# Low parts of the weights by an accumulating DMA instead of a DVE subtraction

## The chip, the core and the metric

The kernel runs on one core of a Trainium2 chip. A core has a matrix engine (TensorE, in the profile PE, with its weight loads as PEld), a vector engine (DVE), a scalar engine (ACT), GpSimd (POOL) and a sync engine (SP) that here only issues transfers. Sixteen DMA engines move data between the device memory and the core's working memory (SBUF). The metric is the device time of one execution in microseconds, lower is better.

## The reference

One layer of a decoder with 512 tokens, 16 meta tokens in front, 1024 channels and 8 heads. Two branches run side by side on the same normalised input, differential softmax attention and a gated delta rule in chunks; their results are projected, gated, added and projected once more.

```python
hn = rms_norm(h, norm_w)
proj = hn @ w_in
aq, ak, av, az, dq, dk, dv, dz, db, da, ga, gd = split(proj)
o_a = diff_attention(aq, ak, av, lam)
y_a = (rms_norm(o_a, attn_norm_w) * (1 - lam_init) * silu(az)) @ w_branch_attn
o_d = gated_delta_chunked(q, k, v, beta, g)      # q, k, v: conv + silu of dq, dk, dv
y_d = (rms_norm(o_d, dn_norm_w) * silu(dz)) @ w_branch_delta
merged = sigmoid(ga) * y_a + sigmoid(gd) * y_d
out = rms_norm(h + merged @ w_out, final_norm_w)
```

All of it is in fp32. `w_in`, the two branch matrices and `w_out` are the weights that this document is about.

## The kernel before

**Products.** The large products run on PE in a format with fewer mantissa bits than fp32 (float32r). To keep the accuracy, both factors are split into a high part, which is the value rounded to that format, and a low part, which is the rest, and three passes are added up: high times high, high times low, low times high (`PASSES`, line 54). So each 128 x 1024 block of weights (512 KB) is needed as two tiles, `wh` and `wl`; for the output projection most of them are called `woh` and `wol`. There are 96 blocks in the order of the list `ORDER` (four groups of two heads, then the gates and the branch projections) and 8 blocks of `w_out`.

**How a block is prepared.** `load_weights(n)` (line 404) takes one of the `raw` tiles and lets SP load the block into it. `split(n, raw)` (line 383) then takes a slot for a pair of split tiles and does two things: ACT copies `raw` to `wh`, which rounds it, and DVE writes `wl` as `raw` minus `wh`. With that the raw tile is given back. The table `SLOTS` (line 64) says how many tiles of each kind exist: three `raw`, two pairs `w`, four pairs `wo`. So a block's copy can start when PE has finished with the block two places earlier, and the next load when a subtraction has ended.

**How a block is used.** `dense()` makes the products in `ORDER`. For each eighth of the depth it issues the three passes one behind the other, so the low part of the weights enters with the third matmul of a block (the second in the first two blocks, which are made by `first_products` as the tokens arrive). `give("w")` at its end frees the pair.

**What sets the order.** The kernel does not leave the order to the compiler. Its parts are generators (tasks), and a planner (`Plan`) runs them on a table of estimated times: the task that can start soonest by that estimate emits its next instruction. The result is one fixed order of instructions for each engine; every engine keeps its order and waits at the first instruction that isn't ready. The estimate of a DMA (`transfer`) counts its bytes once, whatever its kind. What stands around the split on the engines: on ACT the copies out of the accumulators, tanh (`th`), the exponentials (`e`) of the softmax and those of the decays (`E`, `eg`); on DVE the delta rule's triangular inverse, a chain of some thirty pairs `tmps`, `ts` in each of the four groups; on POOL masks (`E`, `ts`), small powers and the copies of `ak` within SBUF; on SP the loads of `raw` and small transfers by way of the device memory (`scrm`, `msub`, `scrt`, `td`, `E` and `eg` from `gcd`).

Every engine instruction is emitted by one helper, so nearly all of them have line 216 in the profile; groups are told apart by their tiles.

Of the kernel before, what the change touches and what calls it, by code (L numbers as in the profile page):

```python
# [10 lines left out]
F32 = mybir.dt.float32  # L11
# [25 lines left out]
def dense_order():  # L37
    """Products with weight blocks of 128 columns, in the order in which they are made."""
    order = []
    for g in range(H // 2):  # L40
        for n in ("dk", "dv", "dq"):
            order += [(n, 2 * g), (n, 2 * g + 1)]
        order += [(n, 2 * g) for n in ("ak", "aq", "az", "av")]
        order += [("dz", 2 * g), ("dz", 2 * g + 1)]
        order += [(n, 2 * g + 1) for n in ("ak", "aq", "az", "av")]
    for g, y in (("gd", "yd"), ("ga", "ya")):
        order += [(g, c) for c in range(AHEAD)]
        for c in range(KB):
            order += [(y, c)] + [(g, c + AHEAD)] * (c + AHEAD < KB)
    return order  # L50
# [4 lines left out]

# how many of the accumulators serve a purpose at most, and how many there are
BANKS = dict(pd=2, pat=2, pdl=2)
# [4 lines left out]

# tiles of each kind, and accumulators, that are in use at a time
SLOTS = dict(raw=3, w=2, wo=4, psc=1, xp=2, y=2, kT=2, qT=2, ktd=2, vr=2, E=2, eg=1, AT=2, MT=2, sc=2, km=1,
             ts=1, msub=1, TT=1, aq=2, ak=1, vT=1, vs=1, e=4, pT=2, pm=2, ao=1, br=8, th=4)


# until when the tensor engine's clock runs at half its rate
COLD = 10500
# [8 lines left out]
class Plan:  # L78
    """Puts the instructions of many tasks in one order, which all engines keep.

    A task is a generator. It yields the engine that its next instructions are for and then emits them; or an event's
    name, to wait for that; or (name,), to wait for one of some slots. The task that can start soonest goes on, by an
    estimate of the instructions' times in ns; of several, the one of the lowest rank.
    """

# [11 lines left out]
    def here(self):  # L97
        """When and where that is done which the running task has emitted."""
        if self.arrival:
            return self.arrival, SP  # L100
        return (self.end, self.engine) if self.engine else (self.task.time, self.task.src)
# [44 lines left out]
    def settle(self):  # L146
        """Lets every task go on that waits for what is there."""
        moved = True
        while moved:
            moved = False  # L150
            for task in sorted(self.tasks, key=lambda t: t.rank):
                if task.want == ():
                    self.wait(task, (0.0, SP))
                elif isinstance(task.want, tuple):
                    kind = task.want[0]
                    free = self.slots["bank" if kind in self.kinds else kind]
                    if not free or self.kinds.get(kind) == 0:
                        continue
                    if kind in self.kinds:
                        self.kinds[kind] -= 1  # L160
                    free.sort()
                    *since, task.slot = free.pop(0)
                    self.wait(task, tuple(since))
                elif task.want in self.events:
                    self.wait(task, self.events[task.want])
                else:
                    continue
                moved = True
# [22 lines left out]
class Banks(list):  # L191
    """The accumulators of a product, in the order in which they are done."""

# [7 lines left out]
class Engine:  # L201
    """An engine whose instructions' times are estimated as they are emitted."""

# [47 lines left out]
def hybrid_block(ctx: ExitStack, tc: tile.TileContext, x, meta, wblk, wbd, wout, pcol, prow, out):  # L251
# [30 lines left out]
    def bank(kind):  # L282
        """An accumulator, two banks for scores, else one: that which the running task has taken."""
        return mk(ps, [P, 2, 512], F32, kind, SLOTS[kind]) if kind == "psc" else banks_[plan.task.slot]

# [15 lines left out]

    # ---------------------------------------------------------------- constants
    nwb = mk(sp, [P, D], F32, "nwb")
# [75 lines left out]

    # ---------------------------------------------------------------- loads  # L380
    weights = {}

    def split(n, raw):
        """Weights as high and low parts."""
        if n < len(ORDER) or n - len(ORDER) in (4, 5):
# [11 lines left out]
        done(f"wh{n}")  # L397
        yield DVE
        V.tensor_tensor(out=wl, in0=raw, in1=wh.bitcast(F32), op=ALU.subtract)
        give("raw")  # L400
        done(f"w{n}")

    def load_weights(n):
# [3 lines left out]
        m = n - len(ORDER)  # L407
        S.dma_start(out=raw, in_=wblk[n] if m < 0 else wout[m // 4, :, m % 4 * D:m % 4 * D + D])
        spawn(split(n, raw), 0.3 if n < 2 else 0)

# [27 lines left out]

    # ---------------------------------------------------------------- hn, transposed, as high and low parts
    hn = [hnp.tile([P, KB, L], F32R, tag=t, name=t) for t in ("hnH", "hnL")]  # L440

    def normalise(n):
        """The meta tokens lie as (part of the channels, token) on the partitions, the others by token."""
        yield f"x{n}"
# [53 lines left out]

    # ---------------------------------------------------------------- gates of the delta rule, all heads
    FULL = [(0, 272), (272, 256)]  # L500
# [11 lines left out]
    def gates():  # L512
# [137 lines left out]
        spawn(rows())  # L650
        # the meta tokens of two heads lie on 32 partitions
        msel = gt("msel", (32, 8, 2))
# [47 lines left out]

    # ---------------------------------------------------------------- what follows a projection
    od = [rp.tile([P, SEQ], F32, tag=f"od{h}", name=f"od{h}") for h in range(H)]
# [10 lines left out]
    def conv_silu(banks, chan, t_lo, dst_tag, tags=("pd", "pd")):  # L713
        """2 silu(conv(projection)) from t_lo on, in a tile of dst_tag or in that returned second, else scratch"""
        n = L - t_lo
# [45 lines left out]
    def after_gate(h, banks, dst, event):  # L761
        """dst = 2 silu(projection)"""
        pd = banks[0][0]
# [85 lines left out]

    # ---------------------------------------------------------------- the delta rule, two heads at a time  # L850
    kt_, s_, sd_, vs_, qe_ = 0, 1, 2, 3, 4

    def delta_pair(gi):
# [14 lines left out]
        def decay(i):  # L868
            """exp(gc_j - gc_i), keys on partitions"""
            h = hs[i]  # L870
# [16 lines left out]
        def keys(i):  # L887
# [23 lines left out]
            def decayed():  # L911
                """The keys' part in the state at the end of their chunk"""
                for c in range(NC):
# [184 lines left out]

        # inverses of the unit triangular 32 x 32 blocks, a block and half its columns on a partition
        yield ("ts",)  # L1100
# [39 lines left out]
        tdt, tdmt = mk(dp, [P, 8, 32], F32, "tdt", 1), mk(dp, [32, 32], F32, "tdmt", 1)  # L1140
        # blocks of 32 to 64 to 128, transposed; x is head and chunk
        TT = slot(dp, [P, 8, P], F32, "TT")
# [213 lines left out]

    # ---------------------------------------------------------------- differential attention, one head
    def attention(h):
# [11 lines left out]
        def combine(i, st, es):  # L1370
# [7 lines left out]
            give("e")  # L1378
            # the meta tokens' part, of which a high part, a high part and a low part lie beside one another
            yield ("pm",)  # L1380
# [118 lines left out]

    # ---------------------------------------------------------------- the dense products  # L1500
    def again(tag, dt=F32):
# [6 lines left out]
    def branch(h, of, name):  # L1508
        """A branch's result as high and low parts."""
        yield f"{'od' if name == 'yd' else 'oa'}{h}"  # L1510
# [42 lines left out]
    def first_products():  # L1553
        """The first two products, in parts that follow the tokens' arrival."""
        yield ("psc",)
# [24 lines left out]
    def dense():  # L1580
        yield from first_products()
        for n, (name, i) in list(enumerate(ORDER))[2:]:
# [28 lines left out]
            if name in ("yd", "ya"):  # L1611
                tick(name, KB)
                if i == KB - 1:
                    for _ in range(H):
                        give("br")
        # the output projection, the residual and the last norm
        yield "gp"
# [24 lines left out]
    def finish(hf, tb, c0, c1, pd, tag, ssq, fnw, xr):  # L1642
        """The residual's sum and its square's; with the last columns of some tokens, their norm"""
        t = xr[hf, tb][:, c0:c1]
# [15 lines left out]
        spawn(weigh(), 2)  # L1660
        # of the sums so far, but the last: mean + eps
        if col == 0:
# [28 lines left out]
    def pools():  # L1691
        """The pools that take the place of those of the two branches."""
        yield "delta"
# [41 lines left out]
def layout(inputs):  # L1735
    """The inputs as the program reads them: moved, and nothing else."""
    f = {k: np.asarray(v) for k, v in inputs.items()}
# [41 lines left out]
```

## Time and profile before

| | |
|---|---|
| device time, median of 3 runs | 787.66 us (786.45 to 788.36) |
| span of the profiled execution (its own time is not given apart from that) | 787.3 us |
| PE busy | 761.1 us |
| DVE, ACT, POOL busy | 541.8, 383.3, 76.1 us |
| moved by DMA | 74.36 MB, 94 GB/s on average |
| loads of weight blocks | 104 of 512 KB |

The span runs from the first to the last instruction of one execution. "Busy" counts the time in which an engine executes; waiting, issuing transfers and semaphores do not count. A row of the waits names the engine and tile that waited and, behind the arrow, what ended the wait; a row of the groups or the timeline names the engine, the operation and out<-in, and in square brackets the idle time of the engine just before it.

### The profile page before, as it was taken

To read this page: it belongs to the slowest core of one execution; us is meant where nothing else is said; L and a number is where in the kernel's file an instruction comes from. 1 tells how busy PE (TensorE), PEld (TensorE's weight loads), DVE (VectorE), ACT (ScalarE), POOL (GpSimd) and SP (SyncE) were. 2 spreads that over 40 slices of the span, in tenths; PEclk is the share of its full clock that TensorE was granted. 3 is DMA by queue.
4 is the path that set the end of the run, shared out by engine and by line. 5 is a ranking of instruction groups with operands and counts; after the bars stand their busy time and mean duration, and the time that the engine had idled before them with its cause. 6 is when DMAs were issued, how large, how long until landed. Compare 5 with 4: busy or idle time off the path is not lost.

```text
span 787.3 us, 13576 instructions
## 1 busy us (share of the span) xinstructions
PE 761.1 (97%) x5191; PEld 682.8 (87%) x5191; DVE 541.8 (69%) x1279; ACT 383.3 (49%) x944; POOL 76.1 (10%) x114
## 2 busy tenths in 40 slices
PE   5999999999999999999999999899999999999996
PEld 4999878999988899987999998788888888888886
DVE  6788697788779778859968875995772334335643
ACT  5374535576545557553557744355562224223322
POOL 3120002021100301100030201000000000000001
PEclk9999999999999999999999999999999999999999
DMA  7132624202352401272240125233116232233402
GB/s 274 40 110 84 152 81 110 68 28 82 95 141 81 122 28 55 67 153 83 81 110 28 56 90 119 81 94 83 51 62 235 80 108 88 100 100 112 136 1 107
DMA packets 46744, 74.36 MB, mean 94 GB/s; under 512 B 20528, under 2 KB 29136, under 8 KB 46680
## 3 DMA queue, kind: packets, MB, share of 16 engines
q1 hardware_dynamic: 45400, 69.18, 29.3%
q0 software_dynamic: 1280, 4.33, 2.5%
q8 instruction: 40, 0.66, 0.3%
q14 instruction: 24, 0.20, 0.1%
HBM read 65.98 MB, written 3.19 MB: 88 GB/s over the span
## 4 chain that ended last, share of the span: by engine, by line
PE 57%; DMA 5%; DVE 4%; issue 1%; ACT 1%; SPq 1%; POOL 1%; POOLq 0%; DVEq 0%; ACTq 0%
PE bank L216 55%; DMA msub<-scrm 2%; PE psc L216 2%; DVE wl L216 1%; DMA scrt<-ts 1%; DMA td<-scrt 1%; SPq L216 1%; DVE tmps L216 1%; DVE ts L216 1%; DMA eg<-gcd 1%; DMA scrm<-MT 1%; DVE aq L216 0%; POOL ts L216 0%; DVE MT L216 0%; ACT wh L216 0%
## 5 line engine op out<-in xcount | busy, mean ns | idle before, releaser
L216 PE MATMUL bank<-hnH,wh 128*128 128x512 f32 (+3 forms) x944 | 317.6, 339 | 1.4 <-ACT hnH L216 0.8
L216 PE MATMUL bank<-hnH,wl 128*128 128x512 f32 (+3 forms) x944 | 302.9, 323 | 3.7 <-DVE wl L216 3.7
L216 PE MATMUL bank<-hnL,wh 128*128 128x512 f32 (+3 forms) x944 | 302.4, 323 | 0.0
L216 PEld LDWEIGHTS bank<-hnH,wl 128*128 128x128 f32 x944 | 177.7, 189 | 19.6 <-DVE wl L216 5.5
L216 PEld LDWEIGHTS bank<-hnH,wh 128*128 128x128 f32 x944 | 177.8, 189 | 15.0 <-ACT hnH L216 1.0
L216 PEld LDWEIGHTS bank<-hnL,wh 128*128 128x128 f32 x944 | 178.0, 190 | 11.1
L216 ACT CAST wh<-raw 128x1024 fp32r<-128x1024 f32 x98 | 102.8, 1049 | 127.0 <-PE bank L216 116.2
L216 DVE TENSOR_TENSOR wl<-raw,wh 128x1024 fp32r<-128x1024 f32 x98 | 120.0, 1225 | 61.4 <-ACT wh L216 60.8
L216 DVE SCALAR_TENSOR_TENSOR y<-xp,pc,y 128x528 f32<-128x528 f32 (+1 forms) x72 | 54.3, 755 | 0.8 <-ACT y L216 0.2
L216 PE MATMUL bank<-brH,wh 128*128 128x512 f32 x128 | 50.1, 392 | 0.0
L216 PE MATMUL bank<-brL,wh 128*128 128x512 f32 x128 | 49.8, 389 | 0.0
L216 PE MATMUL bank<-brH,wl 128*128 128x512 f32 x128 | 49.8, 389 | 0.0
L216 ACT ACTIVATE e<-psc,ast 128x144 f32<-128x144 f32 (+3 forms) x64 | 34.4, 541 | 30.3 <-DVE ast L216 26.2
L216 DVE TENSOR_TENSOR tmps<-msub,ts 97x240 f32<-97x240 f32 (+27 forms) x124 | 39.5, 319 | 5.9 <-DMA msub<-scrm 4.1
L216 DVE TENSOR_TENSOR ts<-ts,tmps 97x240 f32<-97x240 f32 (+27 forms) x124 | 39.6, 320 | 1.8
L216 PE MATMUL psc<-ak,aq 128*128 128x264 f32 (+3 forms) x160 | 29.1, 304 | 4.3 <-ACT e L216 4.3
L216 POOL DMA_DIRECT2D ak<-ak x16 | 8.8, 551 | 219.5 <-DVE ak L216 161.2
L216 PEld LDWEIGHTS psc<-ak,aq 128*128 128x128 f32 x160 | 23.6, 189 | 7.2 <-ACT e L216 6.0
L216 DVE SCALAR_TENSOR_TENSOR od<-th,bank 128x512 f32<-128x512 f32 x16 | 10.9, 684 | 26.6 <-PE bank L216 26.6
L216 DVE TENSOR_REDUCE ast<-psc 128x1 f32<-128x528 f32 (+3 forms) x40 | 28.5, 713 | 0.2
L216 PEld LDWEIGHTS bank<-brH,wh 128*128 128x128 f32 x128 | 24.0, 188 | 5.1
L216 PEld LDWEIGHTS bank<-brH,wl 128*128 128x128 f32 x128 | 24.0, 188 | 5.1
(299 smaller groups left out, 1214.6 us busy)
## 6 DMA issues: line engine op xcount, KB each, us to landing
raw<-in_wblk_dram SPq DMA_DIRECT2D x96, 512.0 KB, 3.5
ak<-ak POOLq DMA_DIRECT2D x16, 264.0 KB, 4.3
raw<-in_wout_dram SPq DMA_DIRECT2D x8, 512.0 KB, 3.7
xt<-in_x_dram SPq DMA_DIRECT2D x4, 512.0 KB, 3.6
E<-gcd SPq DMA_DIRECT2D x8, 256.0 KB, 5.7
eg<-gcd SPq DMA_DIRECT2D x8, 256.0 KB
xr<-in_x_dram SPq DMA_DIRECT2D x8, 256.0 KB, 6.5
out_dram<-xr SPq DMA_DIRECT2D x8, 256.0 KB, 2.1
```

The costliest lines, as they stand in the source:

```text
L216: return real(*args, **kw)
```

## The change

For all blocks but the first two the low part is made in another way. ACT copies `raw` a second time, with a scale of -1, into `wl`, which rounds in the same manner and so leaves the negated high part there. After that POOL issues a DMA from the weights in the device memory onto `wl` that adds (`accum_op=ALU.add`), so `wl` becomes the weight minus its high part. The raw tile is given back after the second copy, before that DMA. The 512 KB of each block are now read from the device memory twice. The table has two `raw` tiles in the place of three and three `w` pairs in the place of two, and the scratch memory for the descriptors of software-issued DMAs is set to 4096 bytes a partition, which makes room for them. The rest of the diff removes comments.

```diff
-SLOTS = dict(raw=3, w=2, wo=4, psc=1, xp=2, y=2, kT=2, qT=2, ktd=2, vr=2, E=2, eg=1, AT=2, MT=2, sc=2, km=1,
+SLOTS = dict(raw=2, w=3, wo=4, psc=1, xp=2, y=2, kT=2, qT=2, ktd=2, vr=2, E=2, eg=1, AT=2, MT=2, sc=2, km=1,
...
-    def split(n, raw):
+    def split(n, raw, src):
...
         wl = mk(pl, [P, D], F32R, f"{kind}l", SLOTS[kind])
         weights[n] = wh, wl
         done(f"wh{n}")
-        yield DVE
-        V.tensor_tensor(out=wl, in0=raw, in1=wh.bitcast(F32), op=ALU.subtract)
-        give("raw")
+        if n < 2:
+            yield DVE
+            V.tensor_tensor(out=wl, in0=raw, in1=wh.bitcast(F32), op=ALU.subtract)
+            give("raw")
+        else:
+            yield ACT
+            A.activation(out=wl, in_=raw, func=AF.Copy, scale=-1.0)
+            give("raw")
+            yield POOL
+            G.dma_start(out=wl, in_=src, accum_op=ALU.add)
         done(f"w{n}")
...
-        S.dma_start(out=raw, in_=wblk[n] if m < 0 else wout[m // 4, :, m % 4 * D:m % 4 * D + D])
-        spawn(split(n, raw), 0.3 if n < 2 else 0)
+        src = wblk[n] if m < 0 else wout[m // 4, :, m % 4 * D:m % 4 * D + D]
+        S.dma_start(out=raw, in_=src)
+        spawn(split(n, raw, src), 0.3 if n < 2 else 0)
...
-    nc = _bacc.Bacc("TRN2", target_bir_lowering=False, num_devices=1)
+    nc = _bacc.Bacc("TRN2", target_bir_lowering=False, num_devices=1, dynamic_dma_scratch_size=4096)
```

Since the planner's estimates change with it, instructions move on all engines. Two places matter below. The first is the last stage, in which only the gates' and the branches' products run. ACT's order there before (`oa` is the high part of the merged branches, `od` their sum):

```order
L216 CAST wh_7664<-raw_7583 128x1024
L216 CAST oa_1133_7672<-od_1039_7072 128x512
L216 CAST wh_7700<-raw_7615 128x1024
L216 ACTIVATE th_7706<-bank_2_79 128x512
L216 CAST wh_7732<-raw_7647 128x1024
```

and now:

```order
L216 CAST oa_1135_7761<-od_1039_7134 128x512
L216 CAST wh_7790<-raw_7738 128x1024
L216 ACTIVATE th_7796<-bank_6_83 128x512
L216 ACTIVATE wl_7792<-raw_7738 128x1024
L216 CAST wh_7823<-raw_7771 128x1024
L216 ACTIVATE wl_7825<-raw_7771 128x1024
L216 CAST oa_1144_7831<-od_1057_7248 128x512
```

The second copy of a block stands behind the tanh of a finished product where there is one. On POOL the same stage, where nothing stood before, is now a row of DMAs, here five of them:

```order
L216 DMA wl_7825<-in_wblk_dram 128x1024
L216 DMA wl_7862<-in_wblk_dram 128x1024
L216 DMA wl_7895<-in_wblk_dram 128x1024
L216 DMA wl_7932<-in_wblk_dram 128x1024
L216 DMA wl_7965<-in_wblk_dram 128x1024
```

The second place is the triangular inverse of the first group, on DVE. Before, a piece of its chain (`ts`, `tmps`), with the subtractions of the weights between:

```order
L216 TENSOR_TENSOR tmps_1166<-msub_108,ts_646 97x87
L216 TENSOR_TENSOR wl_1149<-raw_947,wh_1147 128x1024
L216 TENSOR_TENSOR ts_646<-ts_646,tmps_1166 97x29x3
L216 SCALAR_TENSOR_TENSOR oa_140<-th_1172,bank_2_79 128x512
L216 TENSOR_TENSOR tmps_1196<-msub_108,ts_646 97x112
```

and now the same piece:

```order
L216 TENSOR_TENSOR tmps_1178<-msub_108,ts_619 97x87
L216 TENSOR_TENSOR ts_619<-ts_619,tmps_1178 97x29x3
L216 TENSOR_TENSOR tmps_1186<-msub_108,ts_619 97x112
L216 TENSOR_TENSOR ts_619<-ts_619,tmps_1186 97x28x4
L216 TENSOR_TENSOR tmps_1196<-msub_108,ts_619 97x135
```

The subtraction is gone from the chain, and the gate's product (`oa`) stands a few rows later. On POOL, around the same time, the copies of `ak` and the masks of `E` stood alone before:

```order
L216 DMA ak_1029<-ak_1029 64x1056 x2
L216 AFFINE_SELECT E_1014<-E_1014 128x512
L216 AFFINE_SELECT E_1083<-E_1083 128x512
L216 DMA ak_1600<-ak_1600 64x1056
L216 MEMSET ts_1603 64x512
```

and now stand between the DMAs:

```order
L216 DMA wl_1036<-in_wblk_dram 128x1024
L216 DMA ak_1041<-ak_1041 64x1056
L216 AFFINE_SELECT E_1015<-E_1015 128x512
L216 DMA ak_1041<-ak_1041 64x1056
L216 DMA wl_1118<-in_wblk_dram 128x1024
L216 AFFINE_SELECT E_1095<-E_1095 128x512
L216 DMA wl_1164<-in_wblk_dram 128x1024
```

So a DMA for a low part waits in POOL's queue behind the instructions ahead of it, and they behind it.

## The prediction

> **What bounds the kernel now.** I read the page from the top, then busy time by stage, then the waits of the tensor engine, and last the order of time around its gaps.
>
> ```profile
> span 787.3 us, 13576 instructions
> PE 761.1 (97%) x5191; PEld 682.8 (87%) x5191; DVE 541.8 (69%) x1279; ACT 383.3 (49%) x944; POOL 76.1 (10%) x114
> ...
> PE 57%; DMA 5%; DVE 4%; issue 1%; ACT 1%; SPq 1%; POOL 1%; POOLq 0%; DVEq 0%; ACTq 0%
> ...
> L216 ACT CAST wh<-raw 128x1024 fp32r<-128x1024 f32 x98 | 102.8, 1049 | 127.0 <-PE bank L216 116.2
> L216 DVE TENSOR_TENSOR wl<-raw,wh 128x1024 fp32r<-128x1024 f32 x98 | 120.0, 1225 | 61.4 <-ACT wh L216 60.8
> ```
>
> TensorE (PE) is busy 97% of the span, and its work is not touched: the same products are made from the same two parts. Only the 26 us in which it is not busy can be won back. VectorE (DVE) is at 69%, so the subtractions (120.0 us in the row, 98 at 1225 ns, and six more for the tiles named wol) are a cost only where PE waits for DVE. Busy time by stage says where that can be; the columns are the stretch, then busy time of PE, its weight loads, DVE, ACT and POOL, the clock granted to PE, the DMA engines' busy share and GB/s.
>
> ```profile
> 40.00:550.00 510.00, 499.53 (x3875) 461.58 (x3875) 404.65 (x1024) 282.21 (x761) 59.13 (x85) 0.99 0.32 88
> 550.00:736.00 186.00, 186.00 (x875) 154.49 (x875) 89.40 (x136) 69.83 (x120) 3.02 (x3) 1.00 0.33 108
> 600.00:700.00 100.00, 100.00 (x437) 81.79 (x436) 36.28 (x41) 28.95 (x39) 0.00 (x0) 1.00 0.31 100
> ```
>
> From 550 to 736 us PE has no gap at all: nothing can be gained there, only lost. From 40 to 550 us it lacks 10.5 us. The rest lies in the start and the tail, which the change leaves alone (the first two blocks keep the subtraction).
>
> **Where the gaps are.** First the three worst stretches for a busy DVE (the first three rows), then the same stretches for instructions on the tile wl alone (PE, PEld, DVE), then what PE waited for between 40 and 550 us (total, times, longest).
>
> ```profile
> 100.00:110.00 10.00, 8.10 (x35) 6.47 (x34) 9.83 (x28) 3.12 (x9) 0.00 (x0) 0.83 0.28 95
> 230.00:240.00 10.00, 8.91 (x45) 7.19 (x44) 9.66 (x26) 2.96 (x7) 0.00 (x0) 1.00 0.22 64
> 490.00:510.00 20.00, 17.12 (x95) 14.16 (x94) 19.19 (x52) 7.52 (x18) 0.00 (x0) 1.00 0.25 79
> ...
> 100.00:110.00 10.00, 4.21 (x10) 2.21 (x10) 1.48 (x2) 0.83 0.28 95
> 230.00:240.00 10.00, 4.11 (x11) 1.94 (x11) 2.44 (x2) 1.00 0.22 64
> 490.00:510.00 20.00, 9.50 (x27) 4.97 (x27) 4.14 (x4) 1.00 0.25 79
> ...
> PE psc L216 <- ACT e L216: 4.3, 3, 1.9
> PE bank L216 <- DVE wl L216: 3.7, 4, 1.5
> ```
>
> In these 40 us DVE is 97% busy and PE lacks 1.90 + 1.09 + 2.88 = 5.9 us. In the first stretch the clock was also granted at 0.83, which is worth (1 - 0.83) x 10 = 1.7 us more. The subtractions hold 1.48 + 2.44 + 4.14 = 8.1 us of DVE there.
>
> **Part 1, the subtraction leaves DVE: -5 us.** Removing 8.1 us of DVE where it is the bound, against 5.9 + 1.7 = 7.6 us of PE loss, could win all of the 7.6. I take two thirds, because the work behind it (the softmax's e on ACT, 4.3 us of PE's waits) now stands on an ACT that has more to do. Elsewhere the removal is worth nothing: PE has no gap that DVE ends.
>
> **Part 2, a second pass on ACT and a longer way to the low part.** Each of 102 blocks gets an ACT copy with scale -1. The cast of the same shape takes 1049 ns, so this adds 102 x 1.05 = 107 us, and ACT goes from 49% to 62%. The busy time itself hides behind PE; what counts is the chain from a free slot to a finished low part. In the last stage the chain of before is plain:
>
> ```profile
> 626.68 1.05 ACT L216 CAST wh<-raw 128x1024 fp32r<-128x1024 f32 x1 [4.53 <-PE bank L216]
> 627.64 0.59 ACT L216 ACTIVATE th<-bank 128x512 f32<-128x512 f32 x1
> 627.77 1.23 DVE L216 TENSOR_TENSOR wl<-raw,wh 128x1024 fp32r<-128x1024 f32 x1 [4.36 <-ACT wh L216]
> 632.13 1.05 ACT L216 CAST wh<-raw 128x1024 fp32r<-128x1024 f32 x1 [3.91 <-PE bank L216]
> 632.16 0.39 PE L216 MATMUL bank<-brH,wh 128*128 128x512 f32 x1
> ```
>
> A cast starts when PE has finished with the slot (626.68), and the block is used one product later (632.16). With 437 matmuls in 100 us and 24 in a product, a product takes 5.49 us. With three slots the chain gets two products, 10.98 us, plus 0.45 us because the low part enters with the third matmul. The new chain is cast 1.05, tanh 0.59 (it now stands between the two copies on ACT), negation 1.05, some 0.2 us of hand-overs, and the DMA, so the DMA may take 8.5 us from its issue.
>
> The trace has no accumulating DMA. The nearest rows:
>
> ```profile
> q1 hardware_dynamic: 45400, 69.18, 29.3%
> q0 software_dynamic: 1280, 4.33, 2.5%
> ...
> L216 POOL DMA_DIRECT2D ak<-ak x16 | 8.8, 551 | 219.5 <-DVE ak L216 161.2
> ...
> raw<-in_wblk_dram SPq DMA_DIRECT2D x96, 512.0 KB, 3.5
> ak<-ak POOLq DMA_DIRECT2D x16, 264.0 KB, 4.3
> ...
> DMA to landing us min/median/max: 2.9/4.3/9.8
> ```
>
> The 600 to 700 us row moves 100 GB/s at a share of 0.31, which is 10 MB in 31 us of all 16 engines, so a load of 512 KB (0.524 MB) costs 1.63 us of them. The DMAs issued by POOL (q0, the ak copies from SBUF to SBUF) cost 2.5% of 787.3 us for 4.33 MB, 4.55 us per MB, so 512 KB read from SBUF would be 2.38 us. An accumulation reads the block from memory, reads the tile and writes it. Its bounds: 1.63 us, if the second read is hidden; 1.63 + 2.38 + 2.38 = 6.4 us, if the write back costs as much as the read. I take both reads one behind the other, **4.0 us**, because the software queue's row is the nearest one for the tile's side. Latency: the quickest ak copy landed 2.9 us after its issue, of which 264 KB are 1.2 us, so 1.7 us are fixed; with 4.0 of transfer and 1.63 for the raw load that the same negation sets free on SP, 7.3 us, inside the 8.5. So latency fits in the last stage, and the engines' time does not quite: 1.63 + 4.0 = 5.64 us of DMA per product of 5.49. Over the 25 products from 600 to 736 us that is 25 x 0.15 = **+3.7 us**. At the lower bound it is 0; at the upper, 8.0 us per product, 25 x 2.5 = +63 us.
>
> The Trainium skill, "Collectives: The Full Stack" (Part 3, the bandwidth ceiling), says that an add in the DMA costs nothing by itself and halves the rate because of its two source reads. No run here shows it yet; by that rule the accumulation would be 2 x 1.63 = 3.3 us (an estimate from that page and the load's row), 4.9 us per product, and this term would be 0. That is the first rival below.
>
> **Part 3, four places between 40 and 550 us: +4 us.** At the head of each group of heads ACT stands waiting for a DMA (eg), and the cast behind it is late. The first group, ACT and then PE:
>
> ```profile
> 80.37 0.63 ACT L216 ACTIVATE eg<-eg 128x512 f32<-128x512 f32 x1 [4.97 <-DMA eg<-gcd]
> ...
> 84.11 1.04 ACT L216 CAST wh<-raw 128x1024 fp32r<-128x1024 f32 x1
> 85.05 0.57 ACT L216 CAST aq<-bank 64x512 fp32r<-64x512 f32 x1
> ...
> 86.46 0.40 PE L216 MATMUL bank<-hnH,wl 128*128 128x272 f32 x1 [0.42 <-DVE wl L216]
> ...
> 92.14 0.40 PE L216 MATMUL bank<-hnH,wh 128*128 128x512 f32 x1
> ```
>
> Before, PE waits 0.4 us here. With three slots the cast at 84.11 is that of the next block, first used at 92.14. Its chain: 84.11 + 1.04 + 0.57 + 1.05 + 7.3 = 94.1 us, against 92.14 + 0.46 for the third matmul: 1.5 us late, 1.1 us more than before. Four groups make +4 us. The transfers of eg, E and msub in the same stretch are left out of this; with the slowest landing of an ak copy, 9.8 us, in the place of 7.3, a group loses 3.6 us, so the bound above is +14. Below it is -3.7: PE's waits for DVE wl all go and none comes. The new DMA also stands in POOL's queue, which waits in order: behind it are the masks of E, the blocks of ts and the ak copies, for which ACT and PE wait. POOL is 10% busy and an ak copy holds it for 551 ns, so I cost this at nothing; if its wait for a negation holds a ts mask, the delta chain is late by as much, once a group.
>
> **Part 4, the output weights: +2 us.** Two raw tiles serve the eight blocks that were loaded like this:
>
> ```profile
> 717.23 20.30 SPq L216 DMA_DIRECT2D raw<-in_wout_dram  x8
> ...
> 712.00:741.00 29.00, 29.00 (x129) 23.90 (x128) 19.07 (x23) 12.12 (x14) 0.00 (x0) 1.00 0.54 163
> ```
>
> From 712 to 741 us, when the fourth of them is first needed, the engines work 0.54 x 29 = 15.7 us; five accumulations add 20; about three loads (4.9 us) can move behind. That is 30.8 us in 29. Elsewhere a load lands in 3.5 us (the row above) and a product takes 5.49, so two raw tiles are cover enough while the DMA engines keep up. The smaller descriptor scratch I cost at nothing: a handful of software DMAs is in flight at most.
>
> **Sum.** -5 + 3.7 + 4 + 2 = +4.7 us on a span of 787.3 us. The profile gives no time for that execution but its span; the timed runs have a median of 787.66, 0.4 above it, taken as what lies around. 787.3 + 0.4 + 4.7 = **792 us**.
>
> **Rivals.**
> First, **faster, about 783 us**: the second read is as quick as a load (3.3 us), DMA has 0.6 us per product to spare, the output stage fits, and lateness at the four places shrinks to about a microsecond in all: 787.7 - 5 + 1. For it: full-speed loads exist (512 KB in 1.63). Against: the q0 row is half again as slow per byte. It decides below 5.49 - 1.63 = 3.86 us per accumulation. The skill's rule above is this case. Should all 7.6 us come back, 780.
> Second, **no change, 787.7 +- 2.4**: what DVE gives back and what the longer chain takes cancel; the third tile then only pays for the longer way and buys no lead, so the change does not do what more tiles would say. For it: 186 of the 787 us have no gap to win.
> Third, **far slower, 810 to 850**: the write back is not hidden. Half way to the upper bound an accumulation is 5.2 us, a product 6.8, and 25 x 1.35 = +34 us comes on top of the forecast's 788.7 without its 3.7: about 822. It decides from 3.86 us as well, and also where the latency passes 8.5 us, with half a microsecond per product for each microsecond over.
>
> **Chances.** Forecast (790 to 800) 0.35; faster 0.24; same 0.17; far slower 0.24. A measurement of this kernel tells 0.3% (2.4 us) from no change, so faster 0.24, same 0.17, slower 0.35 + 0.24 = 0.59. For the range I leave out the upper half of the third rival (0.12) and the outermost 0.03 of the first: 779 to 825 us.
>
> **What would show it.** The row of DMAs onto wl, with its time to landing: near 7 us in the last stage if I am right, 5 for the first rival, over 8.5 for the third. The stretch from 600 to 700 us: DMA share near 1.0 and PE with small gaps named after a DMA on wl (forecast), 0.9 or less and no gap (first rival). The stretches at 100, 230 and 490 us: PE's lack should fall from 5.9 us to about 2, and DVE to near 80%. The heads of the groups: PE waiting for a DMA on wl some 1.5 us each. I am wrong in kind if PE waits for ACT in the last stage (the second copy, not the DMA, is then the limit), or if POOL's queue holds the accumulations.

## The result, and the profile after

The changed kernel took 864.43 us (median of four executions, 857.43 to 867.49), the kernel before 788.01 us beside it: a ratio of 1.0947, 95% interval 1.0891 to 1.1003. That is 76 us slower, outside the range of the prediction. Ratios leave out executions that were slow as a whole; medians in us are of all.

First the page of the changed kernel: the span, busy time, the DMA queues, the two rows that replace the subtraction, and DMA issues with their median time to landing.

```profile
span 865.8 us, 13786 instructions
PE 790.1 (91%) x5191; PEld 702.0 (81%) x5191; DVE 433.9 (50%) x1177; ACT 475.9 (55%) x1046; POOL 165.2 (19%) x216
...
q0 software_dynamic: 15968, 57.81, 37.4%
...
L216 POOL DMA_DIRECT2D wl<-in_wblk_dram x94 | 83.0, 883 | 410.8 <-ACT wl L216 293.4
L216 ACT ACTIVATE wl<-raw 128x1024 fp32r<-128x1024 f32 x96 | 101.2, 1055 | 0.0
...
wl<-in_wblk_dram POOLq DMA_DIRECT2D x94, 512.0 KB, 7.8
```

The span grew by 865.8 - 787.3 = 78.5 us, and this splits cleanly on PE. The same 5191 matmuls take 790.1 us in the place of 761.1: **29.0 us**, since the clock was granted at half more often: its mean is 0.952 in the place of 0.994. The means allow at most 0.048 x 865.8 - 0.006 x 787.3 = 36.8 us of lost clock, part of it while PE stood idle, so the 29.0 fit. PE is idle 75.7 us in the place of 26.2: **49.5 us**. DVE did fall, from 541.8 to 433.9 us; all that PE had waited for it on `wl` was 3.7 us. What PE waited for (total, times, longest):

```profile
PE bank L216 <- DMA wl<-in_wblk_dram: 34.7, 8, 9.6
PE bank L216 <- DMA td<-scrt: 11.9, 4, 4.7
PE bank L216 <- DMA wol<-in_wout_dram: 9.5, 4, 4.1
...
PE psc L216 <- ACT e L216: 0.4, 1, 0.4
```

The low parts of the ordinary blocks, those of the output weights, and `td`, a small copy of the delta rule by way of the device memory (1.4 us before). Other engines' waits for transfers rose too. Before, and then in the changed kernel (again total, times, longest):

```profile
ACT eg L216 <- DMA eg<-gcd: 22.6, 8, 5.0
...
DVE E L216 <- DMA E<-gcd: 5.0, 5, 3.1
POOL ts L216 <- DMA scrt<-ts: 4.1, 3, 2.5
```

```profile
ACT eg L216 <- DMA eg<-gcd: 43.4, 8, 6.5
...
POOL ts L216 <- DMA scrt<-ts: 26.1, 3, 9.2
...
ACT wh L216 <- DMA raw<-in_wblk_dram: 18.5, 7, 10.8
DVE E L216 <- DMA E<-gcd: 16.5, 4, 8.3
```

The longest stall is at the head of the third group. Its rows from the timelines of ACT, POOL and PE (start, duration, instruction, in brackets the idle time before it and what ended that):

```profile
373.70 1.05 ACT L216 CAST wh<-raw 128x1024 fp32r<-128x1024 f32 x1
380.47 0.63 ACT L216 ACTIVATE eg<-eg 128x512 f32<-128x512 f32 x1 [5.72 <-DMA eg<-gcd]
381.01 1.04 ACT L216 ACTIVATE wl<-raw 128x1024 fp32r<-128x1024 f32 x1
...
382.36 0.96 POOL L216 DMA_DIRECT2D wl<-in_wblk_dram  x1 [7.02 <-ACT wl L216]
...
393.62 0.80 PE L216 MATMUL bank<-hnH,wl 128*128 128x512 f32 x1 [9.57 <-DMA wl<-in_wblk_dram]
```

The cast is done at 374.75, but the negation of the same block stands behind `eg` in ACT's queue and starts 6.3 us later. The accumulation is issued at 382.4 and PE goes on at 393.6, eleven microseconds later. Busy time of PE in the same place by stretches of 3.4 us (stretch, length and PE busy with its matmuls, granted clock, DMA share, GB/s) shows the rest:

```profile
379.70:383.10 3.40, 3.40 (x31) 1.00 1.06 220
383.10:386.50 3.40, 0.94 (x7) 1.00 1.20 195
386.50:390.00 3.50, 0.00 (x0) 0.51 1.09 181
...
393.40:396.80 3.40, 3.19 (x8) 0.50 0.97 206
```

The DMA engines are full at that moment (`eg`, `E`, `msub`, raw loads and accumulations), and when PE comes back its clock stands at half. The waits for `wl` at the heads of the four groups are 4.39, 4.66, 9.57 and 6.91 us, 25.5 of the 34.7.

The last stage, which the prediction feared, has no gap in its steady part (columns: length, then busy time of PE, PEld, DVE, ACT, POOL; clock, DMA share, GB/s):

```profile
684.00:790.00 106.00, 106.00 (x458) 86.63 (x457) 18.83 (x29) 49.15 (x60) 16.47 (x19) 0.99 0.83 181
```

Just ahead of it is one. There SP loads `xr`, the input for the residual, in eight transfers. The rows are their size and median time to landing (6.5 us before), a cast that waits for the raw load issued behind them, and the wait of PE:

```profile
xr<-in_x_dram SPq DMA_DIRECT2D x8, 256.0 KB, 11.2
...
671.27 1.05 ACT L216 CAST wh<-raw 128x1024 fp32r<-128x1024 f32 x1 [10.75 <-DMA raw<-in_wblk_dram]
...
681.85 0.79 PE L216 MATMUL bank<-hnH,wl 128*128 128x512 f32 x1 [6.04 <-DMA wl<-in_wblk_dram]
```

A last wait for `wl`, of 1.86 us, follows at 796 us.

### The profile page after: what moved, and what is told of

Same layout as the page of the kernel before. It is cut to its first block, busy times and chain, and to the rows that moved or that the text cites. A ratio compares the mean times of both kernels' runs of the same rounds, so it can differ in the third digit from the quotient of the medians.

```text
span 865.8 us, 13786 instructions
## 1 busy us (share of the span) xinstructions
PE 790.1 (91%) x5191; PEld 702.0 (81%) x5191; DVE 433.9 (50%) x1177; ACT 475.9 (55%) x1046; POOL 165.2 (19%) x216
## 3 DMA queue, kind: packets, MB, share of 16 engines
q0 software_dynamic: 15968, 57.81, 37.4%
## 4 chain that ended last, share of the span: by engine, by line
PE 48%; DMA 12%; issue 5%; ACT 2%; DVE 1%; SPq 1%; POOL 0%; POOLq 0%; ACTq 0%
PE bank L216 47%; DMA wl<-in_wblk_dram 3%; DMA scrt<-ts 3%; DMA eg<-gcd 2%; DMA wol<-in_wout_dram 2%; DMA raw<-in_wout_dram 2%; PE psc L216 1%; DMA td<-scrt 1%; SPq L216 1%; ACT wl L216 0%; ACT wh L216 0%; DVE MT L216 0%; ACT wol L216 0%; DVE ts L216 0%; DVE tmps L216 0%
## 5 line engine op out<-in xcount | busy, mean ns | idle before, releaser
L216 PE MATMUL bank<-hnH,wl 128*128 128x512 f32 (+3 forms) x944 | 310.8, 331 | 32.8 <-DMA wl<-in_wblk_dram 32.8
L216 PE MATMUL bank<-hnH,wh 128*128 128x512 f32 (+3 forms) x944 | 325.2, 347 | 3.2 <-ACT ktd L216 2.4
L216 PE MATMUL bank<-hnL,wh 128*128 128x512 f32 (+3 forms) x944 | 308.4, 329 | 0.0
L216 PEld LDWEIGHTS bank<-hnH,wl 128*128 128x128 f32 x944 | 182.6, 194 | 51.0 <-DMA wl<-in_wblk_dram 36.0
L216 PEld LDWEIGHTS bank<-hnL,wh 128*128 128x128 f32 x944 | 182.9, 195 | 12.6
L216 POOL DMA_DIRECT2D wl<-in_wblk_dram x94 | 83.0, 883 | 410.8 <-ACT wl L216 293.4
L216 ACT ACTIVATE wl<-raw 128x1024 fp32r<-128x1024 f32 x96 | 101.2, 1055 | 0.0
L216 DVE SCALAR_TENSOR_TENSOR th<-th,bank 128x512 f32<-128x512 f32 x8 | 5.5, 688 | 54.7 <-PE bank L216 54.7
L216 PE MATMUL bank<-wol,oa 128*128 128x512 f32 (+1 forms) x52 | 20.8, 400 | 9.5 <-DMA wol<-in_wout_dram 9.5
L216 ACT ACTIVATE eg<-eg 128x512 f32<-128x512 f32 x8 | 5.1, 632 | 43.4 <-DMA eg<-gcd 43.4
```

Of the source, the lines that this page charges most:

```text
L216: return real(*args, **kw)
```

## The experiments

The theories. **T1:** order on ACT, the negation stands behind ACT's waits at the group heads. **T2:** the accumulations' traffic on the DMA engines, above all their second read, that of the destination. **T3:** two raw tiles are too few. **The plan:** the planner orders the work by a time for the accumulation that is too short. On top of each, the clock. All ratios below are to the kernel before, beside which each kernel ran.

### The tiles alone

The changed table and scratch, subtraction on DVE for all blocks (`e1_tiles`); and the same with three raw tiles (`e14_sub_raw3_w3`).

```diff
-        if n < 2:
+        if True:
             yield DVE
             V.tensor_tensor(out=wl, in0=raw, in1=wh.bitcast(F32), op=ALU.subtract)
```

> The changed kernel with its three tiles of split weights, two raw tiles and smaller scratch, but with the subtraction on VectorE again for every block. All theories of the cost of the accumulation (ACT's order, the traffic, the clock on top of either) expect 783 to 792, so the 77 us lie in the making of the low part. The theory that two raw tiles are the cause (a load then waits until a tile is free, and comes late) expects over 810 and waits of ACT's wh for raw as long as in the changed kernel (18.5 us in 7).

> The subtraction on VectorE with three raw tiles and three of split weights. With two raw tiles it took as long as before (788.9 against 789.0). All theories: 783 to 790, no difference, since PE waits there for wl in no place.

Measured: 788.87 us, 0.9985 (0.9950 to 1.0019), and 787.29 us, 0.9980 (0.9951 to 1.0009). Tiles and scratch change nothing in either direction; the loss lies in how the low part is made, and a DVE subtraction with more tiles is no gain.

### The second pass without the accumulation

ACT's negated copy stays, but DVE adds the raw tile to it (`e2_dve_add`; with three raw tiles `e6_dve_add_raw3`). In `e15_spare_act`, ACT makes the second pass beside the kernel of before, from `wh` (so it holds no raw tile) onto tiles that nobody reads.

```diff
             A.activation(out=wl, in_=raw, func=AF.Copy, scale=-1.0)
+            yield DVE
+            V.tensor_tensor(out=wl, in0=raw, in1=wl.bitcast(F32), op=ALU.add)
             give("raw")
-            yield POOL
-            G.dma_start(out=wl, in_=src, accum_op=ALU.add)
```

> The changed kernel with the second pass of ScalarE (the negated high part) kept, but the high part's remainder added on VectorE from the raw tile, not by a DMA. Theory T1, that the negation stands behind ACT's waits for eg and E at the group heads: the low parts come late there still, PE waits for wl through DVE instead of DMA, 810 to 850. Theory T2, that the accumulations' traffic on the DMA engines is the cause: 785 to 797, eg back near 5.7 us.

> The kernel with ScalarE's second pass and VectorE's addition (823.6 us with two raw tiles), with three raw tiles. If the second pass costs by the tile it holds: 787 to 800. If it costs by ScalarE's own time (95 us more of it, in front of e, pmT, vT and xp on the same queue): 815 to 828.

> The kernel before with a second pass of ScalarE over each block from n = 2 on, onto spare tiles that nobody reads; the low part is made as before. If ScalarE's own time is what the second pass costs (29 us), by delaying e, pmT, vT and xp behind it: 808 to 820. If the cost was the longer chain from the block to its low part: 786 to 796.

Measured: 1.0391 (1.0303 to 1.0480), 1.0376 (1.0351 to 1.0400) and 1.0039 (1.0010 to 1.0068). So the pass made for the low part costs 29 us and the raw tiles have no share in that (T3 falls for this part), but the pass itself is nearly free. `e6_dve_add_raw3` fell into the range given for ScalarE's own time; `e15_spare_act`, which has that time and hardly any loss, refutes this reading. `e2_dve_add` lies in T1's range, but not by T1's sign: PE waits for `wl` nowhere in it. What is left is the wait for it, or the order that the planner makes when the low part needs it. The next kernel keeps the order of `e6_dve_add_raw3` row for row and takes the wait away (against that kernel):

```diff
-            A.activation(out=wl, in_=raw, func=AF.Copy, scale=-1.0)
+            A.activation(out=spare, in_=raw, func=AF.Copy, scale=-1.0)
             yield DVE
-            V.tensor_tensor(out=wl, in0=raw, in1=wl.bitcast(F32), op=ALU.add)
+            V.tensor_tensor(out=wl, in0=raw, in1=wh.bitcast(F32), op=ALU.subtract)
```

> The order of the kernel with the second pass, VectorE's addition and three raw tiles (817.7 us), row for row, but the second pass goes to a spare tile and VectorE makes the low part from the raw tile and the high part, so that it no longer waits for that pass. If the order costs the 29 us: 812 to 822. If the longer chain's wait does: 787 to 797.

Measured: 818.39 us, 1.0347 (1.0315 to 1.0378). **The order costs it, not the low part's wait for the pass.** (The pass still holds the raw tile, but two raw tiles or three made no difference above.) Of the 30.3 us by which the span is longer than before, 18.0 are busy time of PE, the clock, and 12.3 are idle. The chain of waits that ended last in that kernel, in order of time, at one of the places where the pass stands on it (start, time held, engine, tile):

```profile
277.96 0.41 ACT TT L216
...
281.09 0.95 ACT spare L216
282.04 0.16 ACT S L216
282.21 0.40 ACT TT L216
282.63 0.79 ACT e L216 x2
```

The second pass stands in ACT's queue between the steps of the delta rule (`TT`, `S`) and the softmax's `e`, and so on the chain that ended last; there are four more such places among its longest pieces (from 184, 252, 468 and 535 us). The five hold it for 4.7 us together, so how the order makes up the rest is not shown. In `e15_spare_act`, where nothing hangs on it, the planner put the passes elsewhere, and one stands among the longest pieces.

### The traffic alone

The kernel before, and beside it the same accumulating DMAs onto spare tiles that nobody reads: two tiles (`e3_traffic`), three (`e9_traffic3`), three with plain copies (`e10_plain3`; order row for row that of `e9_traffic3`), and two with ACT's spare pass as well (`e16_both_beside`). The edit is that of `e9_traffic3`, against the kernel before.

```diff
         done(f"w{n}")
+        if n >= 2:
+            yield POOL
+            G.dma_start(out=spare[n % 3], in_=src, accum_op=ALU.add)
```

> The kernel before (three raw tiles, two of split weights, subtraction on VectorE), and beside it, from GpSimd, the same 102 accumulating DMAs of the same blocks from n = 2 on, onto two spare tiles that nobody reads. T2 (traffic alone slows the raw loads and the small copies to and from DRAM): 815 to 860, eg near 9 us and PE's waits on td and ACT's on eg as in the changed kernel. T1 (the order on ACT): 786 to 798.

> The kernel before with the accumulating DMAs beside it that nobody reads, as in the run with two spare tiles (817.7 us), now on three, so that GpSimd waits less for a spare tile (163.9 us of waits there). If the 28 us came from the DMA engines' traffic: 812 to 822 again. If they came from GpSimd's queue, held by an issue that waits for its spare tile: 790 to 802.

> The same, with plain copies of the same blocks onto the three spare tiles instead of accumulating ones. If the second read of each element, that of the destination, makes the traffic dear (4 KB packets of 0.33 us against 0.16): 790 to 802, DMA share about 0.16 lower than beside accumulations. If a second load of each block from DRAM costs by itself, whatever the kind: 810 to 820.

> The kernel before with both beside it, ScalarE's second pass and the accumulations, nobody waiting for either. If the loss of the changed kernel is these two and the low part's own waits (34.7 us on PE, and clock) come on top: 835 to 852. If the two make nearly all of it: 855 to 870.

Measured: 1.0331 (1.0247 to 1.0416), 1.0468 (1.0401 to 1.0536), 1.0123 (1.0071 to 1.0175) and 1.0197 (1.0175 to 1.0219). The queue of GpSimd's DMAs, first in `e9_traffic3`, then in `e10_plain3` (packets, MB, share of the engines' time):

```profile
q0 software_dynamic: 15968, 57.81, 37.4%
```

```profile
q0 software_dynamic: 15968, 57.81, 21.8%
```

The same bytes on the same queue hold the engines for 37.4% of the span as accumulations and for 21.8% as copies, and with nobody waiting for them the first cost 39 us and the second 11. `e3_traffic` came into T2's range, but not by T2's sign: ACT waits 24.6 us for `eg` there, near the 22.6 of before, and not the 43.4 of the changed kernel. `e9_traffic3` lies above both of its ranges. With GpSimd waiting less for a spare tile (114.5 us in the place of 163.9) the loss grew, so it isn't that wait. 13.5 of the 39 us are a single wait of PE for `wh` at 651 us, where ACT had waited 22.1 us for a raw load behind those of `xr`. The sum of the parts failed, though: with both beside it the kernel lost 15 us, less than with the traffic alone, and neither expectation held. What such traffic costs seems to depend on where it falls, which the planner moves with every edit; whether order is all of the difference was not tried.

### The second read, in the changed kernel

Plain DMAs in the place of the accumulating ones; the sum is left out, and every instruction, wait and order stays as in the changed kernel (`e13_plain_in_place`).

```diff
-            G.dma_start(out=wl, in_=src, accum_op=ALU.add)
+            G.dma_start(out=wl, in_=src)
```

> The changed kernel with plain DMAs in the place of the accumulating ones, so that the low part's tile is overwritten with the block and the sum is left out; every wait stays. If the second read is what makes the DMA's traffic dear in the changed kernel (29 to 39 us beside the kernel for accumulations, 10 for plain copies): 830 to 845. If the longer chain and ScalarE's second pass are all: 852 to 866.

Measured: 807.13 us, 1.0242 (1.0209 to 1.0275), beyond the best expectation. Its page and its waits:

```profile
span 805.7 us, 13786 instructions
PE 767.1 (95%) x5191; PEld 685.3 (85%) x5191; DVE 434.1 (54%) x1177; ACT 475.3 (59%) x1046; POOL 131.1 (16%) x216
...
q0 software_dynamic: 15968, 57.81, 21.8%
...
L216 POOL DMA_DIRECT2D wl<-in_wblk_dram x94 | 51.8, 551 | 400.0 <-ACT wl L216 289.1
...
wl<-in_wblk_dram POOLq DMA_DIRECT2D x94, 512.0 KB, 4.8
```

```profile
PE bank L216 <- DMA wl<-in_wblk_dram: 13.3, 4, 6.0
...
PE bank L216 <- DMA wol<-in_wout_dram: 1.0, 2, 0.8
PE bank L216 <- DMA td<-scrt: 0.8, 2, 0.5
```

This is the cleanest pair of the study: one flag of the DMA takes the span from 805.7 to 865.8 us. Of these 60.1 us, 790.1 - 767.1 = 23.0 are the clock and 37.1 idle time of PE. PE's three waits above fall from 56.1 to 15.1 us. The wait for `td`, in whose copy nothing is changed, falls with them (from 11.9 to 0.8), and the stalls of the last stage go. Not all recovers: the four heads of the groups keep 2.56 + 2.64 + 5.99 + 2.12 = 13.3 us of the 25.5, and ACT still waits 35.3 us for `eg` (43.4 with accumulations). So accumulating in the place of copying is worth 57 of the 76 us. That its cause is the second read is an inference: the pair shows the engines' share of the queue (37.4% and 21.8%), not what they do in that time. The rest, 19 us, stays with plain copies: the order, the longer chain and the copies' own traffic, not told apart.

### More lead, another order

Negation in one piece with the cast (`e4_together`), three raw tiles (`e5_raw3`), four pairs of split weights (`e18_w4`), the planner told a time near the measured one (`e8_plan`):

```diff
-    def transfer(self, nbytes):
+    def transfer(self, nbytes, add=False):
...
-        self.dma = max(self.dma, self.hwdge) + nbytes / 360 + 20
-        self.arrival = self.dma + 900
+        self.dma = max(self.dma, self.hwdge) + nbytes / (145 if add else 360) + 20
+        self.arrival = self.dma + (2500 if add else 900)
```

> The changed kernel with the negation emitted in one piece with the cast, so that nothing (eg, E) can stand between them on ACT. T1: the late low parts at 10, 11, 26, 42 and 58 (29 us of PE's stalls) go, and some 20 us of clock with them: 810 to 825. T2: the accumulations still land 10 us after their issue there and the small copies are slow: 845 to 865.

> The changed kernel with three raw tiles in place of two, all else as it is. Theory T3, that each raw tile is now held through two passes of ScalarE, so that with two tiles the next load goes out late: PE's waits for wl halve, ACT's waits for raw (18.5 us) go, 825 to 850. If the raw tiles don't matter (traffic and ACT's load are all): 858 to 870.

> The changed kernel with four tiles of split weights for three, all else as it is. If the accumulation's time on the low part's way is the loss (34.7 us of PE's waits for wl and the clock behind them): 815 to 838, waits for wl under 12 us. If the traffic on the small copies and ScalarE's queue are: 848 to 866, with td and eg waited for as long as before.

> The changed kernel, whose planner is told a time of the accumulation near the measured one (3.6 us of the DMA engines and 2.5 us behind them, for 1.5 and 0.9), so that it places the negations and the work around them by it. If the planner's order by too short a transfer is a cause of the late low parts: 830 to 850. If the time itself is the cause, which no order hides: 858 to 875.

Measured: 876.48 us, 1.1089 (1.0993 to 1.1184); 853.87, 1.0815 (1.0781 to 1.0849); 855.69, 1.0841 (1.0780 to 1.0902); 839.67, 1.0654 (1.0596 to 1.0712). With nothing between cast and negation PE's waits for `wl` did shrink, from 34.7 to 21.7 us, but others came (8.1 us for DVE's `od`, 7.2 for ACT's `vT`) and the kernel became slower, beyond both ranges: T1 as the cause of the loss falls. `e5_raw3` ended between its ranges: ACT's waits for raw tiles fell from 18.5 to 6.4 us, PE's for `wl` only to 28.7. A fourth pair removes the waits for `wl`, and the kernel gains only 9 us, because others come in their place. What PE waited for in `e18_w4`:

```profile
PE bank L216 <- ACT vT L216: 13.5, 5, 6.2
PE bank L216 <- DMA td<-scrt: 13.2, 4, 4.5
PE psc L216 <- ACT e L216: 8.6, 3, 5.0
...
PE bank L216 <- DMA wl<-in_wblk_dram: 0.4, 1, 0.4
```

So more lead for the low part moves the waits and doesn't end them. The planner's truer time is worth 25 us, the largest gain of the four, as its expectation had it.

### Where, and repairs

Accumulation only from n = 66 on (`e7_late_only`), the negation on DVE from the high part, with the raw tile given back behind the cast (`e11_neg_dve`), and that with three raw tiles and the planner's truer time (`e12_repaired`). The edit shown is that of `e11_neg_dve`:

```diff
-            yield ACT
-            A.activation(out=wl, in_=raw, func=AF.Copy, scale=-1.0)
-            give("raw")
+            yield DVE
+            V.tensor_scalar_mul(out=wl, in0=wh.bitcast(F32), scalar1=-1.0)
```

> Accumulation only from n = 66 on, in the last stage and for the output weights (38 of 102 blocks), and the subtraction on VectorE before, all else as in the changed kernel. If the loss lies with the stages whose other work needs ScalarE and the small copies (the four groups, n below 64): 788 to 800, of which some 10 are the output weights' waits. If every accumulation costs alike (77 us over 102 blocks): 815 to 820.

> The changed kernel with the negated high part made on VectorE from the high part (a tensor_scalar, half the elements' time of the subtraction it replaces), so that ScalarE makes the cast alone and gives the raw tile back after it; the accumulation stays. If ScalarE's second pass is worth the 29 us that it costs without the accumulation: 825 to 842. If the accumulation's time to land is all that counts in the changed kernel: 855 to 868.

> The three repairs together: three raw tiles, the planner told the accumulation's time, the negation on VectorE. If the parts found so far add up (864 less 10, 25 and about 29, with some overlap): 800 to 820, and what is left is the accumulations' traffic. If the clock and the late low parts return by another way: over 825. Faster than before (under 786) is not expected by any theory.

Measured: 1.0309 (1.0250 to 1.0368), 1.0642 (1.0590 to 1.0694) and 1.0398 (1.0315 to 1.0480). `e7_late_only` missed the expectation for the groups: it lost 24 us, and its median, 815.84 us, is in the range for a cost that is the same everywhere. But its loss isn't even either. Stretches of it, and PE's waits:

```profile
618.00:624.00 6.00, 0.47 (x3) 0.87 0.98 223
...
630.00:740.00 110.00, 110.00 (x481) 1.00 0.83 179
```

```profile
PE bank L216 <- DMA wl<-in_wblk_dram: 7.9, 3, 5.6
...
PE bank L216 <- DMA wol<-in_wout_dram: 6.8, 4, 2.9
```

The longest stall, with the clock partly at half (0.87), ends at 624 us. The accumulations begin at 546 us, so it is not their start: as in the changed kernel it follows the loads of `xr`, and a cast ahead of it had waited 5.69 us for its raw tile. Behind it are 110 us without a gap, then a wait of 2.1 us for `wl` and those for the output weights. `e11_neg_dve` came into the range by which ACT's second pass counts. `e12_repaired` more than halves the loss, and its median, 822.6 us, lies between its ranges. No version with accumulations came near the kernel before.

## Why the prediction was wrong

**Part 1 (-5 us).** The subtractions left DVE, and PE's waits for DVE `wl`, 3.7 us, went. Those for `e` fell from 4.3 to 0.4 us, but are 3.7 in the same order with plain copies, so that fall isn't owed to the subtractions. Which of the 7.6 us this gave back was not measured apart; it was too small to matter.

**Part 2 (+3.7 us).** In the steady stage the mechanism was judged rightly, its size too dear. By the queue shares an accumulation holds the engines (0.374 x 865.8 - 0.025 x 787.3) / 102 = 2.98 us, where I took 4.0, and a plain copy of the same block (0.218 x 805.7 - 19.7) / 102 = 1.53. Landing is 7.8 us at the median, for 7.3. With 1.63 + 2.98 = 4.6 us per product of 5.49 the steady stage fits: share 0.83, no gap. But the stage cost 6.04 + 1.86 = 7.9 us of waits at its two ends, and the first came behind the loads of `xr`, which this sum of loads and accumulations didn't count. The ratio 2.98 / 1.53 = 1.95 agrees with the Trainium skill, "Collectives: The Full Stack" (Part 3, the bandwidth ceiling), by which an add's two source reads halve the rate.

**Part 3 (+4 us) is the step that failed.** I had four places with one late low part each, 1.5 us late, worked from a cast, a negation right behind it and a landing of 7.3 us, and wrote that the transfers of `eg`, `E` and `msub` were left out of this. Just these are there at the same moment. At the third group the negation came 6.3 us after the cast, behind `eg`, the accumulation landed some 11 us after its issue with the DMA share above 1, and PE stood for 9.57 us. The four places cost 25.5 us of waits for `wl`, above even the bound of 14, and 13.3 of these stay with plain copies, where the chain starts late as well; the other 12.2 go with the slow landing of accumulations on shared engines. The late start goes with the order more than with the traffic, since ACT waits for `eg` 35.3 us with plain copies in place and only 24.6 with the accumulations beside the kernel before. PE also waits 11.9 us for `td`, a copy that the change doesn't touch; I had looked at the low part alone and at the engines' rate only in the stage where it is steady. Accumulating, with its doubled engine time, is worth 57 us in this kernel against plain copies (`e13_plain_in_place`).

**What the sum had no term for.** The clock: 29.0 of the 78.5 us. I counted its loss once, in before, as something to win, and charged none of the stalls that I predicted with the half clock behind them. And the order: I took ACT's added 107 us as hidden because ACT is half idle. The time is hidden (1.0039 beside the kernel), but in the order that the planner makes when the low part hangs on it, a second pass costs 29 us (`e17_order`). That figure is of the kernel without DMAs for the low part; in the changed kernel's own order the pass, the chain and plain copies cost 19 us together.

**Part 4 (+2 us)** was too small: 9.5 us of waits for `wol`, and 1.0 with plain copies.

**POOL's queue and the raw tiles, costed at nothing.** In the trace POOL held an accumulation up to 5.9 us behind the `ts` masks, and no wait of PE for `wl` followed at those places. A third raw tile is worth some 10 us with the accumulations and nothing without.

**The rivals.** The first gave 783 us and decided below 3.86 us per accumulation. That condition was met, at 2.98, and the kernel is slower all the same: the condition looked at the steady stage. Even plain copies in place give 807. The third gave 810 to 850 for a write back of 5.2 us per accumulation in the last stage; its sign was right, its mechanism isn't there.

**What stays open.** Why the same traffic on two spare tiles costs 2.0% with ACT's spare pass beside it and 3.3% without, how the 19 us that remain with plain copies divide between the order, the chain and the copies' traffic, and by what waits the order costs its 29 us.

## What to carry to other kernels

Before work is moved from an engine to the DMA engines, look at the stretches where they are shared with other transfers that something waits for, not at the average nor at the steady stage: 3 us of engine time per block was free there and dear at the four group heads and behind the loads of `xr`. An accumulating DMA cost 1.95 times the engine time of a copy here, and telling the planner a time near the measured one won 25 us. On a kernel that keeps TensorE at 97%, price each expected stall with the half clock that follows it, and test an order by keeping it while the dependence is taken out.

## What the runs showed of the hardware that was not expected

**The clock falls after a stretch that is only partly idle, and can stay low while PE works.** The changed kernel, stretches of 3.4 us (columns as above), and then one place of the kernel before:

```profile
567.40:570.90 3.50, 1.96 (x13) 1.00 0.57 62
570.90:574.30 3.40, 0.29 (x9) 1.00 1.09 259
574.30:577.70 3.40, 3.40 (x36) 0.50 0.10 39
...
584.50:587.90 3.40, 3.40 (x15) 0.50 0.00 0
587.90:591.30 3.40, 3.40 (x41) 1.00 0.73 187
```

```profile
357.70:361.10 3.40, 1.80 (x7) 1.00 0.03 11
361.10:364.50 3.40, 3.40 (x10) 0.50 0.37 143
```

In the second case a stretch with PE busy for 1.80 of 3.40 us was enough, in which PE was never idle for more than 1.19 us at a time; one with 1.96 of 3.50 was not in the first. No limit on the busy share comes out of the traces: 1.85 of 3.40 us was not followed by half clock elsewhere in the kernel before (from 490.8 us), and 3.07 of 3.40 was in `e17_order` (from 276.4 us). Once at half, the clock stayed there for four stretches (the first and the last are shown) in which the profile has PE busy throughout. Many of these matmuls are small ones of the delta rule (32x32 in the timeline), so the profile's busy time may not be what the clock goes by; this is not shown. The Trainium skill, "TensorE: Matmul & The Clock Gate" (Part 1), has the clock fall after an idle window of about 3.4 us and rise after a busy one; the length agrees (the half clock lasts 3.4 us or a multiple), but by the profile's busy time the fall here needs less than an idle window and the rise more than a busy one.

**GpSimd's part of a DMA depends on its kind.** The same 94 issues of 512 KB held POOL for 883 ns each as accumulations and for 551 as plain copies (the rows onto `wl` of the two pages above).
